# Feed-forward products in 2x2 blocks: seven block products in place of eight

## The chip, the cores and the metric

The kernel runs on one core of one Trainium2 chip. The metric is the device time of one execution in microseconds; the median of three runs is given. The engines are TensorE (PE: matrix products; PEld is its weight load), VectorE (DVE), ScalarE (ACT), GpSimd (POOL) and SyncE (SP, which issues most transfers).

## The reference

A sequence of 512 tokens with 1024 features goes through two blocks of two layers each, A and B, then C and D; the second block puts 16 meta tokens in front (528 tokens). Each layer is a mixer (windowed attention, neighbourhood attention, a gated delta rule with short convolutions, windowed attention with meta tokens) and a feed-forward part, each with a residual sum. The change is in the feed-forward part, whose inner width is 2816:

```python
# layers A and B
gu = h @ w_gate_up[i]                                    # h = rmsnorm(x)
x = x + (jax.nn.silu(gu[..., :D_FF]) * gu[..., D_FF:]) @ w_down[i]
# layers C and D
gate, val = jnp.split(h @ w_up, 2, -1)
gate = causal_dwconv(gate, conv_w)                       # 3 taps along the tokens
x = x + (jax.nn.silu(gate) * val) @ w_down
```

All is in float32.

## The kernel before

Features lie on the 128 partitions and tokens along the free axis, so the stream is 8 tiles `X[j]` of 128 features. Every large product is made in three passes: both operands are split into a high part (an ACT copy to fp32r, which rounds) and a low part (DVE, the operand minus its high part), and `mm3` adds high x high, high x low and low x high in PSUM. `wcols` loads a piece of weights, 4 K chunks of 128 rows by 256 columns, into a tile `raw` (3 buffers) through SP's queue; `wpiece` splits it into `hi` and `lo` (4 buffers each) on ACT (L216) and DVE (L217). `kstep` and `linT` run over the K chunks of one output tile of 128 features. A matrix instruction takes up to 512 columns: 512 tokens go in one piece, 528 tokens in two of 264 (`halves`).

`ffn` goes over the 22 chunks f of the inner width in three groups of 8, 8 and 6. A step f (an up step) loads gate and up columns of all 8 K chunks in two pieces, makes the gate tile and the up tile, scales both by the norm's row scale (L290), in C and D applies three taps to the gate (`conv`, L849), applies silu, multiplies both (L883) and splits the result (`split`, L314 and L315) into `ah`, `al`. After a group, its down products are made for 4 pairs of output tiles `jp` and added to the stream (`resid`, L573). In the first step the norm's sums come between the products (`nj.sums`, `nj.rows`), and what was made before them waits in `Held`. In D the first 16 tokens are left out of all but the taps' input, so the gate has two pieces of 258 and 256 columns, and the up and the down products one of 512.

The tile framework places all waits and orders each engine's instructions by a priority (the order of the program) and its own estimate of when operands and buffers are there; on the chip each engine takes its list in order. The slots (`slot`) are 62 buffers of 544 columns that all stages share; `wk` is a ring of five more. During the feed-forward of A, POOL also issues 96 small transfers that lay out the biases of layer B (`load_biases`, L1057).

Of the kernel before, what the change touches and what calls it, by code (L numbers as in the profile page):

```python
# [9 lines left out]
F32 = mybir.dt.float32  # L10
# [15 lines left out]
GROUPS = [(0, 8), (8, 8), (16, 6)]  # L26
# [6 lines left out]
NHI = 4  # L33
NMM = 3
# [7 lines left out]
TAGS = {'t': (3, ['PT'])}  # L42
# [77 lines left out]
def kernel(ctx: ExitStack, tc: tile.TileContext, stop=None, **a):  # L120
# [41 lines left out]
    def col(w, p, bufs=None):  # L162
        bufs = bufs or (6 if w <= 10 else 2)
# [16 lines left out]
    def load_rows(specs, name, mid=False):  # L180
        """vectors of multiples of 128 as columns of a tile"""
# [22 lines left out]
    # ---------------------------------------------------------------- weights and products  # L204
    def wpiece(loads, nk=4, later=None):
        """loads: (partition lo, partitions, chunk lo, chunks, column lo, columns, dram ap [p, c, n]); the split
        in two goes to the list later, if there is one"""
# [3 lines left out]
        hi = wp.tile([P, 4, 256], F32, tag="hi", name=nm("hi"), bufs=NHI)  # L211
        lo = wp.tile([P, 4, 256], F32, tag="lo", name=nm("lo"), bufs=NHI)
        w = max(n0 + nn for _, _, _, _, n0, nn, _ in loads)

        def parts():
            A.activation(r32(hi[:, :nk, :w]), raw[:, :nk, :w], AF.Copy)  # L216
            V.tensor_tensor(r32(lo[:, :nk, :w]), raw[:, :nk, :w], hi[:, :nk, :w], ALU.subtract)  # L217
# [7 lines left out]
    def wcols(w, k0, runs, nk=4, later=None):  # L225
        """K chunks k0.. of a [K, N] weight, columns in runs [(col, n)]"""
# [7 lines left out]
    def wrows64(w, heads, c0):  # L234
        """4 K chunks, each of a pair of 64-row heads"""
# [16 lines left out]
    def mm3(ps, hi, lo, xh, xl, first, last):  # L252
        PE.matmul(ps, r32(hi), r32(xh), start=first, stop=False)  # L253
        PE.matmul(ps, r32(hi), r32(xl), start=False, stop=False)  # L254
        PE.matmul(ps, r32(lo), r32(xh), start=False, stop=last)  # L255
# [19 lines left out]
    def linN(pcs, xs, o, done):  # L275
        """natural: the 128 tokens from o on the partitions, 256 columns"""
# [10 lines left out]

    def scaled(out, rs, dst):
# [3 lines left out]
    class Held:  # L292
        """products whose scale is still to come; two banks leave at once, one waits"""
# [37 lines left out]
    def rms_cols(accs, wins, rhs, y, eps=None):  # L331
        """y[:, (i, j)] = 1/sqrt(mean square + EPS) of the tokens of window j of accs[i]"""
# [37 lines left out]
    def rows_sb(y, T, name):  # L370
        """1/rms of the tokens (columns y) along the free axis of all partitions, in SBUF"""
# [25 lines left out]
    class Norm:  # L397
        """a norm tile by tile: moving operands (x*g) split in two, then sums() gives 1/rms as columns and rows()
        along the free axis"""
# [38 lines left out]
        def sums_edge(self):  # L438
            """also for the windows shifted by half, the last and the first 64 tokens as one"""
# [19 lines left out]
    class Lag:  # L459
        """finished tiles on to the next norm, each after the one that follows it"""  # L460
# [79 lines left out]
    def load_rows_of(src, ntok, mid=None):  # L540
        """[tokens, 1024] as halves of 128 tokens; mid: more loads, after the first half"""
# [10 lines left out]
    def load_T(nat, ntok, out):  # L552
        """the halves of 128 tokens to 8 tiles [128 features, tokens]"""
# [22 lines left out]
    def spill(X, T):  # L576
        """the stream waits in DRAM until the output projection"""
# [1464 lines left out]
```

## Time and profile before

| | |
|---|---|
| median of 3 runs | 2553.25 us (2552.36 to 2562.22) |
| profiled execution: span from first to last instruction | 2552.4 us, the same as the fastest run's time |
| PE busy | 2520.9 us, 99% |
| DVE busy | 1423.0 us, 56% |
| ACT busy | 968.8 us, 38% |
| POOL busy | 275.8 us, 11% |
| feed-forward stages of A, B, C, D, about | 235 to 602, 820 to 1160, 1580 to 1970, 2177 to 2552 us |

Busy time is the time in which an engine has at least one instruction running. Matrix instructions overlap, so what one costs is read from the distance of starts. A duration on DVE or POOL holds what the instruction waited for inside of the engine.

### The profile page before, as it was taken

The numbers are of one execution on the slowest core, as the hardware profiler recorded it, in microseconds if no ns is written. First come the engines' busy times: TensorE is split into PE (matmuls) and PEld (weight loads), VectorE is DVE, ScalarE is ACT, GpSimd is POOL, SyncE is SP. The second block draws the span as 40 slices with busy tenths as digits, with TensorE's granted clock in tenths as the row PEclk, the third lists the DMA queues.
The fourth block names the chain that finished last, engine by engine and source line by source line (L and its number), as shares of the span: only waits on it lengthen the run. The fifth ranks groups of instructions, "written<-read, shape, count | busy, mean of one in ns | idle before, by whom it ended". The sixth has DMA issues, their size and how long they took to land.

```text
span 2552.4 us, 40552 instructions
## 1 busy us (share of the span) xinstructions
PE 2520.9 (99%) x16222; PEld 2203.4 (86%) x16222; DVE 1423.0 (56%) x2838; ACT 968.8 (38%) x1687; POOL 275.8 (11%) x451
## 2 busy tenths in 40 slices
PE   8999999999999999999999999999999999999999
PEld 6788888888887888888888899999999978988887
DVE  7875434347765434347736556545456775645544
ACT  4764322224654323224423233323234664423322
POOL 3127110003130000004312210000000000000000
PEclk9999999999999999999969999999999999999999
DMA  6144333324221323323301123232324222323232
GB/s 191 40 117 98 101 97 91 99 87 129 83 93 58 99 91 91 99 91 92 103 26 34 42 86 91 83 100 83 99 80 126 62 60 59 91 91 100 93 89 75
DMA packets 333648, 224.80 MB, mean 88 GB/s; under 512 B 43939, under 2 KB 324948, under 8 KB 333460
## 3 DMA queue, kind: packets, MB, share of 16 engines
q1 hardware_dynamic: 327524, 211.82, 28.0%
q0 software_dynamic: 5936, 10.39, 1.5%
q8 instruction: 127, 2.08, 0.3%
q14 instruction: 61, 0.50, 0.1%
HBM read 211.21 MB, written 10.86 MB: 87 GB/s over the span
## 4 chain that ended last, share of the span: by engine, by line
PE 47%; DVE 2%; issue 1%; POOL 0%; ACT 0%; POOLq 0%; DVEq 0%; ACTq 0%
PE mm L253 13%; PE mm L254 13%; PE mm L255 13%; PE pso L1874 1%; PE pss L1454 1%; PE pss L1447 1%; PE pss L1859 1%; PE pss L1431 0%; PE pss L339 0%; PE pss L733 0%; PE pss L1433 0%; PE pso L1879 0%; PE pss L734 0%; DVE xt L1420 0%; PE pss L1854 0%
## 5 line engine op out<-in xcount | busy, mean ns | idle before, releaser
L253 PE MATMUL mm<-xh,hi 128*128 128x264 f32 (+3 forms) x2752 | 916.4, 333 | 7.6 <-ACT xh L393 3.2
L254 PE MATMUL mm<-xl,hi 128*128 128x264 f32 (+3 forms) x2752 | 907.7, 330 | 0.5 <-DVE xl L394 0.5
L255 PE MATMUL mm<-xh,lo 128*128 128x264 f32 (+3 forms) x2752 | 906.1, 329 | 0.0
L217 DVE TENSOR_TENSOR lo<-raw,hi 128x1024 fp32r<-128x1024 f32 (+1 forms) x386 | 464.6, 1204 | 344.8 <-ACT hi L216 342.4
L216 ACT ACTIVATE hi<-raw 128x1024 fp32r<-128x1024 f32 (+1 forms) x386 | 400.2, 1039 | 660.6 <-PE mm L254 579.8
L253 PEld LDWEIGHTS mm<-xh,hi 128*128 128x128 f32 x2752 | 523.2, 190 | 61.7 <-issue 7.5
L254 PEld LDWEIGHTS mm<-xl,hi 128*128 128x128 f32 x2752 | 523.5, 190 | 47.2 <-DVE xl L394 1.3
L255 PEld LDWEIGHTS mm<-xh,lo 128*128 128x128 f32 x2752 | 523.3, 190 | 47.5 <-issue 0.5
L254 PE MATMUL mm<-al,hi 128*128 128x512 f32 (+1 forms) x880 | 308.0, 350 | 0.1
L253 PE MATMUL mm<-ah,hi 128*128 128x512 f32 (+1 forms) x880 | 308.0, 350 | 0.0
L255 PE MATMUL mm<-ah,lo 128*128 128x512 f32 (+1 forms) x880 | 307.8, 350 | 0.0
L573 DVE TENSOR_TENSOR xr<-mm,xr 128x264 f32<-128x264 f32 (+1 forms) x168 | 90.5, 542 | 188.0 <-PE mm L255 187.9
L254 PEld LDWEIGHTS mm<-al,hi 128*128 128x128 f32 x880 | 165.5, 188 | 23.1 <-DVE al L315 0.3
L253 PEld LDWEIGHTS mm<-ah,hi 128*128 128x128 f32 x880 | 165.6, 188 | 22.8
L255 PEld LDWEIGHTS mm<-ah,lo 128*128 128x128 f32 x880 | 165.4, 188 | 22.6
L290 DVE TENSOR_TENSOR gt<-mm,rs 128x512 f32<-128x512 f32 (+3 forms) x128 | 66.3, 518 | 185.5 <-PE mm L255 184.4
L877 ACT ACTIVATE gt<-gt 128x512 f32<-128x512 f32 x44 | 27.8, 632 | 176.6 <-DVE gt L290 176.4
L314 ACT ACTIVATE ah<-ut 128x512 fp32r<-128x512 f32 (+1 forms) x88 | 56.0, 636 | 86.3 <-DVE ut L883 86.3
L846 ACT ACTIVATE cy<-gt,fwcol 128x528 f32<-128x528 f32 (+1 forms) x44 | 32.1, 731 | 147.9 <-DVE gt L290 145.5
L254 PE MATMUL mm<-ol,hi 128*128 128x512 f32 (+1 forms) x256 | 87.6, 344 | 0.0
L255 PE MATMUL mm<-oh,lo 128*128 128x512 f32 (+1 forms) x256 | 87.4, 343 | 0.0
L290 DVE TENSOR_TENSOR ut<-mm,rs 128x512 f32<-128x512 f32 (+1 forms) x108 | 63.7, 590 | 42.2 <-PE mm L255 40.5
(485 smaller groups left out, 3195.2 us busy)
## 6 DMA issues: line engine op xcount, KB each, us to landing
raw<-in_w_gate_up_dram SPq DMA_DIRECT2D x176, 256.0 KB, 3.2
raw<-in_ffn_w_up_dram SPq DMA_DIRECT2D x176, 256.0 KB, 3.4
raw<-in_w_down_dram SPq DMA_DIRECT2D x40, 512.0 KB, 3.4
raw<-in_ffn_w_down_dram SPq DMA_DIRECT2D x40, 512.0 KB, 3.4
raw<-in_mix_w_in_dram SPq DMA_DIRECT2D x28, 512.0 KB, 4.0
raw<-in_w_in_b_dram SPq DMA_DIRECT2D x20, 512.0 KB, 3.6
xr<-xd POOLq DMA_DIRECT2D x16, 264.0 KB, 3.9
raw<-in_w_mem_kv_dram SPq DMA_DIRECT2D x8, 512.0 KB, 3.4
```

The costliest lines, as they stand in the source:

```text
L216: A.activation(r32(hi[:, :nk, :w]), raw[:, :nk, :w], AF.Copy)
L217: V.tensor_tensor(r32(lo[:, :nk, :w]), raw[:, :nk, :w], hi[:, :nk, :w], ALU.subtract)
L253: PE.matmul(ps, r32(hi), r32(xh), start=first, stop=False)
L254: PE.matmul(ps, r32(hi), r32(xl), start=False, stop=False)
L255: PE.matmul(ps, r32(lo), r32(xh), start=False, stop=last)
L290: V.tensor_tensor(dst[:, o:o + n], ps[:, :n], rs[:, o:o + n], ALU.mult)
L314: A.activation(r32(dst_h), src, AF.Copy)
L573: V.tensor_tensor(X[j][:, o:o + n], ps[:, :n], X[j][:, o:o + n], ALU.add)
L846: A.activation(out[:, lo:T], src[:, lo:T], AF.Copy, scale=taps[-1])
L877: A.activation(gt[:, w], gt[:, w], AF.Silu)
L1447: PE.matmul(py[q, h], am[q, h], x[q, h], start=True, stop=True)
L1454: PE.matmul(pzt[q, h], y[q, h], xt[q, h], start=True, stop=True)
```

## The change

With the input in two halves of its features (rows of blocks) and two halves of its tokens (columns), and the weights of a gate tile and an up tile in two halves of K, an up step is a 2x2 product of blocks. It is made by seven block products in place of eight, with sums of blocks before and behind (Winograd's form: four sums of weight blocks, four of input blocks, seven of results). `seven` loads the weights of a step into two `raw` tiles, makes four sums on POOL and splits seven blocks into high and low parts. `Blocks` holds the operands of the other side: `first` and `second` take a chunk of the upper and of the lower half and make four sums (on POOL for the input of the up products, `xb`; on DVE for the activations, `zb`) and seven splits. Each block product is 4 K chunks (3 in the down products) times three passes of 256, 258 or 264 columns. `blocks_to` makes an up step's two tiles, `blocks_add` adds a pair of down tiles to the stream; both keep two sums in PSUM by accumulating a second product onto the first.

The input of the block products is normed beforehand (`normed`), so they need the row scale; the first three steps of each stage (`NPLAIN`) are plain, and the block operands are made during them. Groups are now 6, 6, 6 and 4 chunks, and the down products of a group come after the first up step of the next; those of the last group are plain. The biases of layer B are laid out in DRAM through SP's queue (16 transfers) and loaded as 6 tiles, and the memory keys and values of layer B wait in DRAM until then; small column tiles have 4 buffers where they had 6.

```diff
-GROUPS = [(0, 8), (8, 8), (16, 6)]
+GROUPS = [(0, 6), (6, 6), (12, 6), (18, 4)]
...
+NQT = 3
+NPLAIN = 3
...
-TAGS = {'t': (3, ['PT'])}
+TAGS = {'t': (3, ['PT', 's1', 's2', 's4'])}
...
+    def seven(loads, nk):
+        r0, r1 = [wp.tile([P, 4, 256], F32, tag="raw", name=nm("raw"), bufs=NRAW) for _ in range(2)]
+        for r, ld in zip((r0, r1), loads):
+            for n0, nn, src in ld:
+                nc.sync.dma_start(r[:, :nk, n0:n0 + nn], src)
+        v = lambda t: t[:, :512].rearrange("p (k c) -> p k c", c=P)[:, :nk, :]
+        s1, s2, s4 = [v(slot(x)) for x in ("s1", "s2", "s4")]
+        a_, b_ = (slice(None), slice(0, nk), slice(0, P)), (slice(None), slice(0, nk), slice(P, 256))
+        G.tensor_tensor(s1, r0[b_], r1[b_], ALU.add)
+        G.tensor_tensor(s2, s1, r0[a_], ALU.subtract)
+        G.tensor_tensor(r0[b_], r0[a_], r0[b_], ALU.subtract)
+        G.tensor_tensor(s4, r1[a_], s2, ALU.subtract)
+
+        res = {}
+        for keys, srcs in (((1, 5), (r0[a_], s1)), ((6, 7), (s2, r0[b_])), ((2, 4), (r1[:, :nk, :],)), ((3,), (s4,))):
+            h, l = [wp.tile([P, 4, 256], F32, tag=x, name=nm(x), bufs=NHI) for x in ("hi", "lo")]
+            for i, src in enumerate(srcs):
+                w = slice(i * P, i * P + src.shape[2])
+                split(h[:, :nk, w], l[:, :nk, w], src)
...
+    class Blocks:
...
+        def first(self, k, z):
+            h, l = slot(self.tag), slot(self.tag)
+            v = self.win(z)
+            split(self.part(h, 0), self.part(l, 0), v[:, 0, :])
+            self.eng.tensor_tensor(v[:, 0, :], v[:, 1, :], v[:, 0, :], ALU.subtract)
+            split(self.part(h, 1), self.part(l, 1), v[:, 0, :])
...
+        def second(self, k, z):
+            v, t = self.win(z), self.raw[k]
+            h, l = slot(self.tag), slot(self.tag)
+            split(self.both(h), self.both(l), v)
...
+            self.eng.tensor_tensor(t, v[:, 1, :].unsqueeze(1).to_broadcast([P, 2, self.n]), t, ALU.subtract)
+            h, l = slot(self.tag), slot(self.tag)
+            split(self.both(h), self.both(l), t)
...
+            self.eng.tensor_tensor(v[:, 0, :], v[:, 0, :], t[:, 0, :], ALU.subtract)
+            h = slot(self.tag)
+            split(self.part(h, 0), self.part(h, 1), v[:, 0, :])
...
+    def product(ps, i, ws, bl, more=False):
+        w, b = ws[i], bl.ops[i]
+        for k, ((hi, lo), (h, l)) in enumerate(zip(w, b)):
+            mm3(ps[:, :bl.n], hi, lo, h, l, not more and k == 0, k == len(w) - 1, more)
...
+    def blocks_to(ws, bl, c1, c2):
+        n = bl.n
+        (c11, c12), (c21, c22) = [[c[:, bl.o + i * n:bl.o + (i + 1) * n] for i in range(2)] for c in (c1, c2)]
+        pa, pd = mmps(), bank("s")
+        p1, u2 = [quarter("u")[:, :n] for _ in range(2)]
+        product(pa, 1, ws, bl)
+        A.copy(p1, pa[:, :n])
+        product(pd, 5, ws, bl)
+        A.copy(c22, pd[:, :n])
+        pb = bank("s")
+        product(pb, 6, ws, bl)
+        V.tensor_tensor(u2, pb[:, :n], p1, ALU.add)
+        pc = bank("o")
+        product(pc, 7, ws, bl)
+        V.tensor_tensor(c21, pc[:, :n], u2, ALU.add)
+        G.tensor_tensor(c22, c22, c21, ALU.add)
+        product(pa, 2, ws, bl, more=True)
+        A.copy(c11, pa[:, :n])
+        pe = mmps()
+        product(pe, 4, ws, bl)
+        V.tensor_tensor(c21, pe[:, :n], c21, ALU.add)
+        product(pd, 3, ws, bl, more=True)
+        V.tensor_tensor(c12, pd[:, :n], u2, ALU.add)
...
+    def blocks_add(ws, bl, x1, x2):
...
+        V.tensor_tensor(x22, pd[:, :n], x22, ALU.add)
...
+        V.tensor_tensor(u2, pb[:, :n], p1, ALU.add)
...
+        V.tensor_tensor(w, pc[:, :n], u2, ALU.add)
+        G.tensor_tensor(xb2, xb2, w.unsqueeze(1).to_broadcast([P, 2, n]), ALU.add)
+        G.tensor_tensor(x12, x12, u2, ALU.add)
+        product(pa, 2, ws, bl, more=True)
+        V.tensor_tensor(x11, pa[:, :n], x11, ALU.add)
...
+        V.tensor_tensor(x21, pe[:, :n], x21, ALU.add)
...
+        V.tensor_tensor(x12, pd[:, :n], x12, ALU.add)
...
     def ffn(X, T, nj, wgu, wd, taps, done, lo=0, mid=None):
...
+        lb = max(0, lo - 4)
+        xb = Blocks(4, lb, (T - lb) // 2, "xb", G)
+
+        def normed(k, rs):
+            z = wk("xn")
+            V.scalar_tensor_tensor(z[:, :T], X[k][:, :T], gcol(nj.key, k), rs[:, :T], ALU.mult, ALU.mult)
+            return z
...
+        def up(f, put):
...
+            if f < NPLAIN:
...
+            else:
+                ws = seven([kcols(wgu, 4 * h, 4, [(c, P), (DFF + c, P)]) for h in range(2)], 4)
+                blocks_to(ws, xb, gt, ut)
...
+            put(gt, ut)
+            if f < 2:
+                for k in (2 * f, 2 * f + 1):
+                    xb.first(k, normed(k, state["rs"]))
+                    xb.second(k, normed(k + 4, state["rs"]))
+
+        def down(gi, acts):
...
+                if isinstance(acts, Blocks):
+                    ws = seven([kcols(wd, k0, nk, [(jp * 256, 256)]) for k0 in (f0, f0 + nk)], nk)
+                    blocks_add(ws, acts, X[2 * jp], X[2 * jp + 1])
+                    continue
...
+        before = None
+        for gi, (f0, fn) in enumerate(GROUPS):
+            nk = fn // 2
+            acts = [] if gi == len(GROUPS) - 1 else Blocks(nk, lo, (T - lo) // 2, "zb", V)
...
+            for i in range(fn):
+                up(f0 + i, lambda gt, ut: put(gt, ut, i))
+                if i == 0 and before:
+                    down(*before)
+            before = gi, acts
+        down(*before)
...
+        td = dp.tile([P, 6 * 512], F32, name="TBd")
+        for cc in range(16):
+            nc.sync.dma_start(td[8 * cc:8 * cc + 8, :].rearrange("p (i j) -> p i j", j=32),
+                              scap(15 - cc, [[4608, 8], [48, 96], [1, 32]]))
+            if cc > 1:
+                yield
         for hp in range(6):
-            t = slot("TB")
-            for cc in range(16):
-                G.dma_start(t[8 * cc:8 * cc + 8, :512].rearrange("p (i j) -> p i j", j=32),
-                            scap(hp * 768 + 15 - cc, [[4608, 8], [48, 16], [1, 32]]))
-            TB.append(t)
-            yield
+            TB.append(slot("TB"))
+            nc.sync.dma_start(TB[hp][:, :512], td[:, hp * 512:(hp + 1) * 512])
+        memory_back()
```

## Rows read from the trace of the kernel before

**Rows 1.** The page, part 1: busy time, share of the span and instructions.
```profile
PE 2520.9 (99%) x16222; PEld 2203.4 (86%) x16222; DVE 1423.0 (56%) x2838; ACT 968.8 (38%) x1687; POOL 275.8 (11%) x451
```

**Rows 2.** Windows, feed-forward stages of A, C and D: busy time, instructions, clock, DMA.
```profile
245.00:602.00 357.00, 357.00 (x1549) 290.19 (x1548) 161.64 (x190) 105.96 (x126) 34.21 (x69) 1.00 0.35 102
...
1580.00:1970.00 390.00, 389.87 (x3205) 389.14 (x3204) 210.11 (x329) 127.91 (x160) 4.10 (x8) 1.00 0.32 95
...
2177.00:2552.00 375.00, 370.82 (x2115) 322.74 (x2113) 189.42 (x261) 112.85 (x140) 0.00 (x0) 1.00 0.30 89
```

**Rows 3.** Timeline of PE: starts of 15, 40 and 31 products, first and last.
```profile
599.62 0.39 PE L254 MATMUL mm<-al,hi 128*128 128x512 f32 x1
...
602.84 0.39 PE L253 MATMUL mm<-xh,hi 128*128 128x512 f32 x1
...
626.64 0.28 PE L282 MATMUL mm<-hi,xh 128*128 128x256 f32 x1
...
631.27 0.28 PE L282 MATMUL mm<-hi,xh 128*128 128x256 f32 x1
...
1699.81 0.29 PE L255 MATMUL mm<-ah,lo 128*128 128x264 f32 x1
...
1703.48 0.29 PE L255 MATMUL mm<-ah,lo 128*128 128x264 f32 x1
```

**Rows 4.** Groups of DVE by line and form: count, busy us, mean ns.
```profile
L217 DVE TENSOR_TENSOR lo<-raw,hi 128x1024 fp32r<-128x1024 f32 x368 | 452.4, 1230 | 344.8 <-ACT hi L216 342.4 <-PE mm L284 2.0 <-DMA hwcol<-in_swa_q_norm_w_dram 0.2
...
L315 DVE TENSOR_TENSOR al<-ut,ah 128x512 fp32r<-128x512 f32 x66 | 45.2, 685 | 4.2 <-ACT ah L314 4.2
...
L849 DVE SCALAR_TENSOR_TENSOR cy<-gt,fwcol,cy 128x512 f32<-128x512 f32 x44 | 33.1, 752 | 17.9 <-ACT cy L846 17.2
```

**Rows 5.** Timeline of DVE in a step of A: start us, duration us.
```profile
414.45 0.69 DVE L883 TENSOR_TENSOR ut<-ut,gt 128x512 f32<-128x512 f32 x1
415.06 1.22 DVE L217 TENSOR_TENSOR lo<-raw,hi 128x1024 fp32r<-128x1024 f32 x1
416.19 0.68 DVE L315 TENSOR_TENSOR al<-ut,ah 128x512 fp32r<-128x512 f32 x1
```

**Rows 6.** POOL: a group by form, and one line (min, median, max ns).
```profile
L1351 POOL TENSOR_TENSOR tg<-csts,gg 128x512 f32<-128x512 f32 x4 | 4.1, 1038 | 0.9 <-PE pss L1476 0.9
...
L1443 POOL TENSOR_TENSOR am<-ac,lev x23: 308/731/1701, 1266.9 to 1479.4; 128x256 f32<-128x256 f32 x20, 16x64 f32<-16x64 f32 x3
```

**Rows 7.** Timeline of POOL and of DVE from 1206 us, and line L849 (min, median, max).
```profile
1208.13 12.87 POOL L538 TENSOR_TENSOR xc<-xc,r 128x512 f32<-128x512 f32 x8 [8.85 <-ACT r L534]
...
1206.93 8.27 DVE L849 SCALAR_TENSOR_TENSOR qkv<-cg,cwcol,qkv 128x527 f32<-128x527 f32 x6 [0.19 <-ACT qkv L846]
1215.12 0.76 DVE L290 TENSOR_TENSOR cg<-mm,rs 128x264 f32<-128x264 f32 x2
1216.68 3.17 DVE L849 SCALAR_TENSOR_TENSOR qkv<-cg,cwcol,qkv 128x527 f32<-128x527 f32 x2 [0.81 <-ACT qkv L846]
1219.77 0.42 DVE L290 TENSOR_TENSOR cg<-mm,rs 128x264 f32<-128x264 f32 x1
1220.11 1.45 DVE L849 SCALAR_TENSOR_TENSOR qkv<-cg,cwcol,qkv 128x525 f32<-128x525 f32 x1
...
L849 DVE SCALAR_TENSOR_TENSOR qkv<-cg,cwcol,qkv x36: 745/762/1794, 1206.9 to 1333.2; 128x527 f32<-128x527 f32 x12, 128x526 f32<-128x526 f32 x12, 128x525 f32<-128x525 f32 x12
```

**Rows 8.** Timeline, stage A: its first product, and the row scale's copy.
```profile
234.80 0.40 PE L253 MATMUL mm<-xh,hi 128*128 128x512 f32 x1
...
247.76 0.57 ACT L379 COPY rs<-pss 128x512 f32<-128x512 f32 x1
```

**Rows 9.** Groups of ACT by line and form.
```profile
L216 ACT ACTIVATE hi<-raw 128x1024 fp32r<-128x1024 f32 x368 | 389.2, 1059 | 647.3 <-PE mm L254 566.5 <-issue 49.4 <-PE mm L283 18.2
...
L314 ACT ACTIVATE ah<-ut 128x512 fp32r<-128x512 f32 x66 | 41.8, 633 | 45.3 <-DVE ut L883 45.3
```

**Rows 10.** The page, part 6: issues, KB each, median us to landing.
```profile
raw<-in_w_gate_up_dram SPq DMA_DIRECT2D x176, 256.0 KB, 3.2
```

More of the change, by code (lines that the diff above doesn't have):

```diff
@@ L210, in wpiece @@
             nc.sync.dma_start(raw[p0:p0 + pn, c0:c0 + cn, n0:n0 + nn], src)
-        hi = wp.tile([P, 4, 256], F32, tag="hi", name=nm("hi"), bufs=NHI)
-        lo = wp.tile([P, 4, 256], F32, tag="lo", name=nm("lo"), bufs=NHI)
+        hi, lo = [wp.tile([P, 4, 256], F32, tag=x, name=nm(x), bufs=NHI) for x in ("hi", "lo")]
         w = max(n0 + nn for _, _, _, _, n0, nn, _ in loads)
         def parts():
-            A.activation(r32(hi[:, :nk, :w]), raw[:, :nk, :w], AF.Copy)
-            V.tensor_tensor(r32(lo[:, :nk, :w]), raw[:, :nk, :w], hi[:, :nk, :w], ALU.subtract)
+            split(hi[:, :nk, :w], lo[:, :nk, :w], raw[:, :nk, :w])
         if later is None:
@@ L250, in wrows64, with mm3 @@
         return wpiece(loads)
[L252 to L255, printed above, removed]
+    def mm3(ps, hi, lo, xh, xl, first, last, more=False):
+        PE.matmul(ps, r32(hi), r32(xh), start=first, stop=False, skip_group_check=more)
+        PE.matmul(ps, r32(hi), r32(xl), start=False, stop=False, skip_group_check=more)
+        PE.matmul(ps, r32(lo), r32(xh), start=False, stop=last, skip_group_check=more)
     def kstep(out, pcs, k, t, xs, first, last):
@@ L286, in linN @@
         done(ps)
+    def seven(loads, nk):
[16 more added lines that the diff above has]
+                split(h[:, :nk, w], l[:, :nk, w], src)
+            for i, key in enumerate(keys):
+                res[key] = [(h[:, k, i * P:(i + 1) * P], l[:, k, i * P:(i + 1) * P]) for k in range(nk)]
+        return res
@@ L766, in memory_kv, with memory_back @@
                 yield from linN(pcs, xs, t * P, done)
+            if li:
+                d = dp.tile([5 * P, 512], F32, name="memd")
+                for i, t in enumerate([x for pair in kst for h in pair for x in [h[2]]] + [vs]):
+                    nc.sync.dma_start(d[i * P:(i + 1) * P, :], t[:, :512])
+                memK.append(d)
+                memV.append(None)
+                continue
             memK.append(kst)
             memV.append(vt)
+    def memory_back():
+        d = memK[1]
+        t = [slot("memb") for _ in range(5)]
+        for i, x in enumerate(t):
+            nc.sync.dma_start(x[:, :512], d[i * P:(i + 1) * P, :])
+        memK[1] = [[(t[2 * i + hh][:, :256], t[2 * i + hh][:, 256:512]) for hh in range(2)] for i in range(2)]
+        memV[1] = [t[4][:, :256], t[4][:, 256:512]]
     def out_proj(piece, get, T, done, early):
@@ L849, in conv, with kcols @@
             V.scalar_tensor_tensor(out[:, o:T], src[:, o - d:T - d], taps[n - 1 - d], out[:, o:T], ALU.mult, ALU.add)
+    def kcols(w, k0, nk, runs):
+        out, at = [], 0
+        for c, n in runs:
+            out.append((at, n, w[k0 * P:(k0 + nk) * P, c:c + n].rearrange("(c p) n -> p c n", p=P)))
+            at += n
+        return out
     def ffn(X, T, nj, wgu, wd, taps, done, lo=0, mid=None):
@@ L854, in ffn @@
         lg = max(0, lo - 2)
-        for gi, (f0, fn) in enumerate(GROUPS):
-            acts = []
-            for f in range(f0, f0 + fn):
-                c = f * P
-                if mid is not None and f >= MID and (f - MID) % MSTEP == 0:
-                    next(mid, None)
+        w = slice(lo, T)
+        lb = max(0, lo - 4)
[4 more added lines that the diff above has]
+            return z
+        state = {}
+        def up(f, put):
+            c = f * P
+            if mid is not None and f >= MID:
+                next(mid, None)
+            gt, ut = wk("gt"), wk("ut")
+            if f < NPLAIN:
                 pcs = [wcols(wgu, 4 * h, [(c, P), (DFF + c, P)]) for h in range(2)]
-                gt, ut = wk("gt"), wk("ut")
-                w = slice(lo, T)
                 if f == 0:
@@ L889, in ffn, with put @@
                     j = 2 * jp + t
-                    fin = done if gi == len(GROUPS) - 1 else resid(X)
-                    run(linT(pcs, t, acts, T, lambda out, j=j, fin=fin: fin(j, out), fn, lo=lo, wide=j == 0))
+                    run(linT(pcs, t, acts, T, lambda out, j=j: done(j, out), fn, lo=lo, wide=j == 0))
+        before = None
+        for gi, (f0, fn) in enumerate(GROUPS):
+            nk = fn // 2
+            acts = [] if gi == len(GROUPS) - 1 else Blocks(nk, lo, (T - lo) // 2, "zb", V)
+            def put(gt, ut, i):
+                if isinstance(acts, list):
+                    ah, al = slot("ah"), slot("al")
+                    V.tensor_tensor(ut[:, w], ut[:, w], gt[:, w], ALU.mult)
+                    split(ah[:, w], al[:, w], ut[:, w])
+                    acts.append((ah, al))
+                elif i < nk:
+                    z = slot("z")
+                    V.tensor_tensor(z[:, w], ut[:, w], gt[:, w], ALU.mult)
+                    acts.first(i, z)
+                else:
+                    V.tensor_tensor(ut[:, w], ut[:, w], gt[:, w], ALU.mult)
+                    acts.second(i - nk, ut)
+            for i in range(fn):
[4 more added lines that the diff above has]
+        down(*before)
     def dump(X, T, off=0):
```

68 lines of the change are left out of this document (50 added, 18 removed).

## The prediction

> **What bounds the kernel now.** I read the page's busy shares first: TensorE (PE) is busy 99% of the span of 2552.4 us, VectorE (DVE) far less [rows 1]. Shares mix stages, so next the windows by stage: in the feed-forward stages of the layers A, C and D, PE is busy for the whole window, while DVE is busy 162 of 357 us in A and 210 of 390 us in C, and GpSimd (POOL) 34 and 4 us [rows 2]. The stage of layer B looks like that of A. So PE sets the pace in exactly the stages that are rewritten, and DVE has slack. What a product costs is the distance of starts in the matmul timeline, not its duration, since they overlap: 14 steps of 512 columns in 3.22 us, 0.230 each; 39 steps of 256 columns in 4.63 us, 0.119 each; 30 steps of 264 columns in 3.67 us, 0.1223 each [rows 3]. So narrow products cost per column nearly what wide ones do, and halving the width loses 3%, not more.
>
> **What it removes on PE.** One up step (two output tiles, 8 K chunks, three passes) has 48 products of 512 columns in A and B, 48 x 0.230 = 11.04 us. The block form has 7 x 4 x 3 = 84 of 256 columns, 84 x 0.119 = 9.97. In C, 96 x 0.1223 = 11.74 becomes 84 x 0.1223 = 10.27. In D, half are pairs of some 257 columns: 24 x 0.230 + 48 x 0.119 = 11.23 becomes 84 x 0.119 = 9.97. 19 of 22 steps change. A pair of output tiles of a down group of 6 chunks has 36 x 0.230 = 8.28 us (C: 72 x 0.1223 = 8.80); the block form has 63 products, 7.48 (C: 7.70). There are 12 such pairs. PE work saved: A and B 19 x 1.07 + 12 x 0.80 = 29.9 us each, C 19 x 1.47 + 12 x 1.10 = 41.1, D 19 x 1.26 + 9.6 = 33.5; 134 us in all. This would be the gain if PE stayed the bound.
>
> **What it adds, in an up step.** Every block sum and every split now goes through DVE, ScalarE (ACT) and POOL. On DVE I count what one instruction adds to a run of them: 512 columns 0.61 us and 1024 columns 1.13 (starts at 414.45, 415.06, 416.19 [rows 5]), where the durations are 0.685 and 1.23 [rows 4]; 256 columns 0.34 (two evacuations of 0.42 in 0.76 us [rows 7]). The weights need low parts of five 512-column blocks and one of 1024: 5 x 0.61 + 1.13 = 4.18, before 2.26. The gate times up product is 0.61 as before. The activations' block operands take, over a pair of chunks, three times 256 in the first half, and three times 512 and two times 256 in the second: (1.02 + 2.51) / 2 = 1.77, before 0.61. That is 6.56 us of DVE instructions with both inputs in SBUF. Four evacuations of 256 columns from PSUM add 1.36. POOL gets four sums of 512 columns at 1.04 and one of 256 at 0.73 [rows 6]: 4.89, where it had nothing.
>
> **Why these two sums add up.** DVE and POOL look like two engines in parallel, each below PE's 9.97. The trace says they are not, for these instructions. From 1208 us POOL runs eight sums of 512 columns back to back (1.04 alone) while DVE has tap instructions of two SBUF inputs (0.75 alone): DVE's stretch up to 1.79, 0.75 + 1.04, and POOL's eight take 12.87 us instead of 8.3 [rows 6, 7]. Seven taps begin in those 12.87 us (of the first six the two before 1208.13 don't count), and each is 0.08 shorter in a run: 7 x 0.67 + 8 x 1.04 = 13.0. So one holds the other up, and the sum of both is the time. The three PSUM evacuations in there kept 0.42 and cost nothing [rows 7]. So a step takes at least 6.56 + 4.89 = 11.45 us (floor), and 12.81 if no evacuation lies under POOL (in line). Before: 11.04. The seventh of PE's work is saved, and DVE with POOL becomes the bound.
> By the Trainium skill (SBUF — State Buffer, Who interferes with whom) a DVE instruction with two SBUF inputs and a GpSimd one that reads SBUF exclude each other for the whole instruction, and one with a single SBUF input is left alone. The trace agrees but for 0.08 us of a DVE instruction. With full durations the floor would be 12.3 us. The same skill (GPSIMD Engine Reference, Engine selection) sends elementwise sums to VectorE; the rows give 0.61 there against 1.04, so the placement on POOL takes 2.1 us more of the shared time in a step than needed.
>
> **The sum by stage**, floor / middle / in line. I take the middle: the evacuations rode free in the one stretch shown, but here the DVE also has to wait for PE's last product of a step.
> Up, A and B: 11.45 / 12.13 / 12.81 against 11.04. C adds two taps of 0.75: 13.0 / 13.7 / 14.4 against 11.74. D: 12.95 / 13.6 / 14.3 against 11.23. In the last four steps the activations are split plainly, 1.16 us less. Of the 19 steps 15 are full.
> Down, a pair of tiles with 3 + 3 chunks: widths 384 and 768 aren't in the trace; between the rows they take 0.475 and 0.87 on DVE, 0.89 on POOL. DVE 5 x 0.475 + 0.87 = 3.25, POOL 4 x 0.89 + 1.04 + 0.73 = 5.33, floor 8.58; six evacuations 2.04, in line 10.62; middle 9.6. Against 8.28 (C 8.80).
> A and B: 15 x 1.09 - 4 x 0.07 + 12 x 1.32 = +32 us each (bounds 15 x 0.41 - 4 x 0.75 + 12 x 0.30 = +7 and 15 x 1.77 + 4 x 0.61 + 12 x 2.34 = +57). C: 15 x 1.96 + 4 x 0.80 + 12 x 0.80 = +42 (+17 to +68). D: 15 x 2.40 + 4 x 1.24 + 12 x 1.32 = +57 (+32 to +82).
> Start of each stage: the block operands of the input need the norm's row scale, which lands 13.5 us into the stage (234.80 to 248.33 [rows 8]). Three plain steps, 33.1 us and some 2 for the norm's sums, end 21.5 us later. In these lie, for each of four pairs of chunks, DVE 2 x 0.75 + 0.68 + 1.56 and POOL 0.73 + 1.04 + 0.73, 6.2 us, so 25; and 7.1 of the plain steps' own (weights 2.26, products 3 x 0.61, first block operands 3 x 1.02). 32.1 in 21.5 leaves the first block product 10.6 us late; 42 us in four stages. Bounds 4 and 20 each, by how far the chain from ACT to DVE to POOL and back overlaps.
> Sum: 2 x 32 + 42 + 57 + 42 = +205; bounds 2 x 7 + 17 + 32 + 16 = +79 and 2 x 57 + 68 + 82 + 80 = +344.
>
> **What I cost at nothing.** ACT: a step has five splits at 0.63, one at 1.06 [rows 9], three copies of 256 columns, the activation and 1.2 of operands, under 8 us in a step of 12. DMA: the weights' bytes and issues in the changed steps are the same, and a load lands in 3.2 us [rows 10]; without that cover it is the rival on buffers. The biases of layer B go by a DRAM tile on SP's queue, not POOL's, and five tiles of memory keys and values go to DRAM and back: all of it inside stage A, whose buffers would have to run dry for it to count. Fewer small column tiles: a wait between tiny instructions, below 1 us each in attention. The last group of four chunks is plain in its down products and costs what it did.
>
> **Rivals.** 1. POOL's sums don't hold DVE up (the pair in the rows shared more than the port, say, or POOL reads these blocks quickly). Then PE stays the bound in all steps: DVE alone needs 7.9 of 9.97 us in A and 9.5 of 10.27 in C. 134 us less, some 3 us lost at each start: 2552 - 134 + 12 = 2430. For it: the page's shares, and DVE's slack. Against: 1.79 us taps. It decides once a sum holds DVE up for about 0.28 us less than the 0.94 it takes on average: 95 + 72 + 12 sums in each stage, 716 in all, and 205 / 716 = 0.29 brings the time back to before.
> 2. It cancels: sums below the floor in A and B by overlap, above in C and D, within 0.5%.
> 3. Buffers bind as well. Three raw tiles serve two per step, and the first is held until its difference has been split. From its release to that of the next: the load 3.2, three POOL sums at 1.04 with a DVE instruction of 0.61 before each, 4.95, the high part 0.63, the low part 0.61 behind a POOL sum of 1.04: 10.4 us, and then the wait for a high/low tile that PE still reads. Four such tiles are one step's set. If this adds 1.9 us to 76 steps and 1.5 to 48 pairs, 2757 + 216 = 2970.
>
> **How the numbers follow.** The profiled execution's span is 2552.4, next to the fastest run's 2552.36 and 0.85 below the median of 2553.25, so the sum is one on the median within 1 us: 2552.4 + 205 = 2757. Chances: shared port as bound, 2631 to 2896, 0.72; a little below that and still slower 0.04; rival 3 0.08; rival 1 0.11; rival 2 0.05. Faster by over 0.5% (about what a measurement of this kernel can tell from no change) 0.11, within it 0.05, slower 0.84. The range goes from 2570 to 2970, which leaves out rival 1, rival 2 and half of rival 3; the likeliest one's own is 2631 to 2896.
>
> **What would show it.** Right: in the feed-forward windows PE's busy share falls well below 1, PE waits for DVE's low parts; POOL's sums of 512 columns last well over 1.04 and DVE's splits over 0.69 on average; DVE plus POOL busy comes close to the window. An up step in the middle of A takes 11.5 to 12.8 us, in C 13.0 to 14.4; some 10 us of idle PE before the first block product. Wrong, if matmuls of 256 columns don't start 0.119 us apart when fed, if POOL's sums keep 1.04 beside DVE's splits, or if PE waits for loads.

## The result, and the profile after

The changed kernel takes 2859.52 us in the median of four runs (2851.23 to 2865.14), against 2552.81 for the kernel before on the same chip: a ratio of 1.1189, 95% interval 1.1156 to 1.1222. The forecast was 2757 us, slower with a chance of 0.84, and a range of 2570 to 2970. Sign and mechanism held. The size was half as large again, +307 in place of +205, between the middle and the upper bound (+344).

The page of the changed kernel, part 1, answers to [rows 1]:
```profile
PE 2542.0 (89%) x18454; PEld 2316.2 (81%) x18454; DVE 2204.5 (77%) x3981; ACT 1321.9 (46%) x2663; POOL 1164.6 (41%) x1071
```
PE fell from 99% to 89%. PE's busy time did not fall although its work did. At least part of the reason is half clock, which makes a matmul count as busy for longer: at about 440.5 us, where the granted clock falls from 2.4 to 1.2 GHz, the duration of a 256-column matmul goes from 0.28 to 0.41 us and the distance of starts from 0.12 to 0.22, and the mean granted clock of the whole execution went from 0.986 to 0.949. The windows of the four feed-forward stages, A to D, show where it waits, and answer to [rows 2] (columns as there: PE, PEld, DVE, ACT, POOL busy, clock, DMA share, GB/s):
```profile
245.00:690.00 445.00, 376.11 (x2622) 350.73 (x2622) 354.58 (x518) 196.45 (x375) 252.22 (x231) 0.94 0.32 94
897.00:1335.00 438.00, 371.00 (x2621) 343.72 (x2619) 382.66 (x524) 203.36 (x397) 253.71 (x193) 0.96 0.27 79
1765.00:2190.00 425.00, 346.66 (x2555) 333.06 (x2556) 366.17 (x514) 197.12 (x367) 228.17 (x177) 0.94 0.28 82
2404.00:2863.00 459.00, 383.77 (x2715) 358.90 (x2714) 386.98 (x551) 205.32 (x386) 235.98 (x179) 0.94 0.25 75
```
PE has gone from the whole window to 82 to 85% of it, DVE from about half to 80 to 87%, POOL from next to nothing to more than half. What PE waits for, in the list of waits (total us, times, longest us):
```profile
PE pss L255 <- DVE lo L451: 83.6, 65, 4.6
PE mm L255 <- DVE lo L451: 75.3, 48, 3.7
```
So it waits for the low parts that DVE makes. The groups of DVE and of POOL by form (count, busy us, mean ns) answer to [rows 4] and [rows 6]:
```profile
L451 DVE TENSOR_TENSOR lo<-raw,hi 128x1024 fp32r<-128x1024 f32 x228 | 284.5, 1248 | 67.9 <-ACT hi L450 60.7 <-DMA raw<-in_w_out_dram 6.5 <-PE mm L255 0.5
L451 DVE TENSOR_TENSOR lo<-s,hi 128x512 fp32r<-128x512 f32 x228 | 219.6, 969 | 17.7 <-ACT hi L450 15.9
L451 DVE TENSOR_TENSOR lo<-raw,hi 128x512 fp32r<-128x512 f32 x154 | 185.0, 1202 | 9.2 <-ACT hi L450 7.5
L386 DVE TENSOR_TENSOR ut<-pso,u 128x256 f32<-128x256 f32 x38 | 15.9, 417 | 3.3 <-PE pso L255 1.8
```
```profile
L305 POOL TENSOR_TENSOR s<-raw,s 128x512 f32<-128x512 f32 x76 | 126.7, 1667 | 5.7 <-ACT zb L450 3.4 <-DVE lo L451 2.3
L304 POOL TENSOR_TENSOR raw<-raw 128x512 f32<-128x512 f32 x76 | 126.0, 1657 | 0.0
```
The low parts of 512 columns, 0.685 us in [rows 4], now take 0.97 to 1.20 on average; the evacuations, with one input in PSUM, keep 0.417; POOL's sums, 1.04 in [rows 6], take up to 1.67. One place in stage B shows how a mean of 1.2 comes about; first the timeline of DVE, then that of POOL over the same stretch (start us, us):
```profile
1078.55 0.69 DVE L352 TENSOR_TENSOR z<-ut,z 128x512 f32<-128x512 f32 x1
1079.28 0.69 DVE L451 TENSOR_TENSOR zb<-ut,zb 128x512 fp32r<-128x512 f32 x1
1080.00 1.41 DVE L357 TENSOR_TENSOR ut<-ut,z 128x256 f32<-128x256 f32 x1
1081.33 1.78 DVE L451 TENSOR_TENSOR zb<-z,zb 128x512 fp32r<-128x512 f32 x1
1083.04 1.48 DVE L451 TENSOR_TENSOR zb<-ut,zb 128x256 fp32r<-128x256 f32 x1
1084.44 0.41 DVE L383 TENSOR_TENSOR u<-pss,u 128x256 f32<-128x256 f32 x1
```
```profile
1079.36 1.77 POOL L302 TENSOR_TENSOR s<-raw,raw 128x512 f32<-128x512 f32 x1 [4.63 <-DVE z L352]
1081.20 1.36 POOL L303 TENSOR_TENSOR s<-s,raw 128x512 f32<-128x512 f32 x1
1082.53 1.71 POOL L304 TENSOR_TENSOR raw<-raw 128x512 f32<-128x512 f32 x1
1084.20 1.44 POOL L305 TENSOR_TENSOR s<-raw,s 128x512 f32<-128x512 f32 x1
```
(The bracket is the engine's idle time before the row and what ended it.) Here a DVE instruction with two SBUF inputs that finds a sum running takes up to 1.1 us longer than without one: 512 columns 1.78 in place of 0.69, 256 columns 1.48 in place of the 0.42 that the same line takes at 440.12 us, where no sum runs. The one at 1079.28, which runs already when the first sum starts, keeps its 0.69, and the sum takes 1.77. While the four sums run, the two engines take turns. The last row, an evacuation, meets a sum as well and keeps its 0.41.

Two windows of four up steps each in stage B, and one of a whole group there (six up steps and four pairs of down tiles, from one gate activation to that six later):
```profile
1064.60:1116.40 51.80, 43.55 (x314) 42.05 (x315) 50.09 (x62) 25.52 (x53) 28.10 (x20) 0.90 0.25 75
1182.00:1234.00 52.00, 41.35 (x324) 39.08 (x324) 50.36 (x62) 25.48 (x52) 27.53 (x20) 1.00 0.25 74
...
1052.10:1169.30 117.20, 100.45 (x756) 95.37 (x756) 104.76 (x138) 52.18 (x105) 72.47 (x54) 0.96 0.28 81
```
An up step takes 12.95 and 13.0 us on average, a little over the upper bound of the prediction (12.81), and DVE is busy for 97% of it: held, but with hardly a gap. The clock was 0.90 in one window and 1.00 in the other, and the time is the same, so half clock doesn't set the pace in these windows.

### The profile page after: what moved, and what is told of

Its sections match the earlier page's. It is cut to its first block, busy times and chain, and to the rows that moved or that the text cites. A ratio compares the mean times of both kernels' runs of the same rounds, so it can differ in the third digit from the quotient of the medians.

```text
span 2863.1 us, 48858 instructions
## 1 busy us (share of the span) xinstructions
PE 2542.0 (89%) x18454; PEld 2316.2 (81%) x18454; DVE 2204.5 (77%) x3981; ACT 1321.9 (46%) x2663; POOL 1164.6 (41%) x1071
## 4 chain that ended last, share of the span: by engine, by line
PE 38%; DVE 31%; POOL 10%; issue 10%; ACT 5%; DMA 5%; SPq 0%; POOLq 0%; DVEq 0%; ACTq 0%
DVE lo L451 12%; PE mm L253 8%; PE mm L254 7%; PE mm L255 7%; DVE zb L451 4%; POOL s L302 2%; POOL s L303 2%; POOL raw L304 2%; ACT hi L450 2%; DMA raw<-in_ffn_w_down_dram 2%; DVE cy L1002 1%; POOL s L305 1%; DVE z L1085 1%; PE pss L869 1%; PE pss L255 1%
## 5 line engine op out<-in xcount | busy, mean ns | idle before, releaser
L451 DVE TENSOR_TENSOR lo<-raw,hi 128x1024 fp32r<-128x1024 f32 (+3 forms) x526 | 591.9, 1129 | 82.9 <-ACT hi L450 72.8
L450 ACT ACTIVATE hi<-raw 128x1024 fp32r<-128x1024 f32 (+3 forms) x526 | 422.1, 813 | 273.0 <-PE mm L254 107.5
L451 DVE TENSOR_TENSOR lo<-s,hi 128x512 fp32r<-128x512 f32 (+1 forms) x372 | 328.8, 890 | 63.8 <-ACT hi L450 62.0
L253 PE MATMUL mm<-xh,hi 128*128 128x264 f32 (+3 forms) x1080 | 362.3, 336 | 15.5 <-DVE gt L425 4.4
L254 PE MATMUL mm<-xl,hi 128*128 128x264 f32 (+3 forms) x1080 | 352.9, 327 | 0.7 <-DVE xl L530 0.6
L255 PE MATMUL mm<-xh,lo 128*128 128x264 f32 (+3 forms) x1080 | 351.3, 326 | 0.0
L253 PE MATMUL mm<-xb,hi 128*128 128x256 f32 (+2 forms) x912 | 267.1, 293 | 42.8 <-ACT u L378 27.9
L253 PE MATMUL pss<-xb,hi 128*128 128x256 f32 (+2 forms) x912 | 272.6, 299 | 30.9 <-ACT hi L450 15.8
L254 PE MATMUL pss<-xb,hi 128*128 128x256 f32 (+2 forms) x912 | 270.2, 296 | 2.8 <-DVE xb L451 2.6
L254 PE MATMUL mm<-xb,hi 128*128 128x256 f32 (+2 forms) x912 | 263.8, 289 | 2.2 <-DVE xb L451 2.2
L254 PEld LDWEIGHTS mm<-xl,hi 128*128 128x128 f32 x1080 | 210.7, 195 | 15.6 <-DVE xl L530 2.5
L255 PEld LDWEIGHTS mm<-xh,lo 128*128 128x128 f32 x1080 | 210.5, 195 | 14.2 <-issue 0.5
```

The source lines that it names most:

```text
L253: PE.matmul(ps, r32(hi), r32(xh), start=first, stop=False, skip_group_check=more)
L254: PE.matmul(ps, r32(hi), r32(xl), start=False, stop=False, skip_group_check=more)
L255: PE.matmul(ps, r32(lo), r32(xh), start=False, stop=last, skip_group_check=more)
```

## The experiments

All are edits of the changed kernel, except the two whose names begin with "before". "Group in B" is the group shown last, at its own place in each trace.

| kernel | us, median | profiled span | group in B |
|---|---|---|---|
| before | 2552 | 2552.4 | 99.4 by PE's terms of the prediction |
| the changed kernel | 2859.5 | 2863.1 | 117.2 |
| sums_dve | 2697.2 | 2686.1 | 102.4 |
| results_dve | 2846.8 | 2851.6 | 117.5 |
| no_sums | 2520.9 | 2519.1 | 88.6 |
| lone_sums | 2941.8 | 2939.6 | 124.5 |
| narrow | 2606.6 | 2586.9 | 95.5 |
| raw4 | 2800.8 | 2794.7 | 112.5 |
| both_dve | 2671.0 | 2672.9 | 99.0 |
| sums_dve_spread | 2662.1 | 2656.8 | 103.2 |
| best | 2600.7 | 2591.9 | 98.9 |
| best_b | 2552.0 | 2543.7 | 97.3 |
| before_pool4 | 2755.2 | 2752.4 | |
| before_dve4 | 2587.3 | 2585.6 | |

My theory was the shared time of DVE and POOL; the rivals were the order of POOL's list (the sums of the next step wait there behind the addition to `c22`, which waits for the seventh product), the raw buffers, and half clock.

**sums_dve.** The weight sums move to VectorE.
```diff
-        G.tensor_tensor(s1, r0[b_], r1[b_], ALU.add)
+        V.tensor_tensor(s1, r0[b_], r1[b_], ALU.add)
...
```
(and the same for the three sums below it)

> The four sums of the weight blocks of seven run on VectorE in place of GpSimd; the output stays the reference's. Shared-time theory (GpSimd's sums and VectorE's tensor-tensor work hold each other up, so that their times add): the sums cost VectorE about 0.7 us each in place of the 1.27 to 1.67 us that GpSimd takes, and the subtractions of split go back from 0.97-1.2 us to about 0.7, so a step of the up-projection falls from some 13.5 to about 11.5 us: total 2600 to 2720. Rival, GpSimd's order (the sums wait in GpSimd's list behind the addition to c22, and the splits wait for the sums): the sums no longer queue there, so the time falls as well, to about 2650 to 2720; lone_sums tells the two apart. Rival, half clock (the losses are stretches at half clock that any stall causes): falls less, 2780 to 2850.

162 us come back, more than half of the loss, ratio to before 1.0572 (1.049 to 1.0654). The group of low parts from sums is back at its old duration:
```profile
L451 DVE TENSOR_TENSOR lo<-s,hi 128x512 fp32r<-128x512 f32 x228 | 156.4, 697 | 0.0
```

**results_dve.** Only the additions to result quarters move to VectorE, so that nothing in POOL's list waits for a product.
```diff
-        G.tensor_tensor(c22, c22, c21, ALU.add)
+        V.tensor_tensor(c22, c22, c21, ALU.add)
...
-        G.tensor_tensor(xb2, xb2, w.unsqueeze(1).to_broadcast([P, 2, n]), ALU.add)
-        G.tensor_tensor(x12, x12, u2, ALU.add)
+        V.tensor_tensor(xb2, xb2, w.unsqueeze(1).to_broadcast([P, 2, n]), ALU.add)
+        V.tensor_tensor(x12, x12, u2, ALU.add)
```


> The additions of result quarters (c22 in the up-projection, xb2 and x12 in the down-projection) run on VectorE in place of GpSimd; the output stays the reference's. GpSimd's list then holds nothing that waits for a product. Shared-time theory: 0.3 to 0.5 us a step come back at most, 2810 to 2850. Rival, GpSimd's order (the next step's four weight sums stand behind the addition to c22, which waits for the seventh product): the sums start when their load lands, 1 to 2 us a step earlier, and the time falls to 2650 to 2750.

13 us, and a group in B of 117.5 against 117.2. The order of POOL's list is worth these 13 us at most.

**no_sums.** The sums are left out; raw blocks stand in for them.
```diff
-        for keys, srcs in (((1, 5), (r0[a_], s1)), ((6, 7), (s2, r0[b_])), ((2, 4), (r1[:, :nk, :],)), ((3,), (s4,))):
+        for keys, srcs in (((1, 5), (r0[a_], r1[b_])), ((6, 7), (r1[a_], r0[b_])), ((2, 4), (r1[:, :nk, :],)), ((3,), (r0[a_],))):
```


> The four sums of the weight blocks are left out: the seven products take raw blocks in their place, so that the seven products no longer make up the reference's product. Everything else, splits and loads and result sums, stays. Shared-time theory: without the sums VectorE has some 10 us of a step and TensorE some 10 as well, so the time is near 2450 to 2520, faster than before. Rival, raw buffers or stage starts bind by themselves (a load of 3.2 us, then splits, from only three buffers): stays above 2600. Rival, half clock: depends on stalls that go away with the sums, 2430 to 2550.

2520.9, just above what was expected (2450 to 2520). Its group in B is bound by PE, at 88.6 us against 6 x 9.97 + 4 x 7.48 = 89.7 by the prediction's PE terms, so the price of the products was right:
```profile
962.40:1051.00 88.60, 88.60 (x750) 88.60 (x750) 77.11 (x138) 51.90 (x105) 14.77 (x14) 1.00 0.37 108
```
Even with no weight sums at all the seven products gain only 1.2% over before (ratio 0.9880, 0.9827 to 0.9933).

**lone_sums.** POOL makes the same sums, and nothing reads them.
```diff
+        s3 = v(slot("s1"))
...
-        G.tensor_tensor(r0[b_], r0[a_], r0[b_], ALU.subtract)
+        G.tensor_tensor(s3, r0[a_], r0[b_], ALU.subtract)
...
```
(and the sources of the splits as in no_sums)

> GpSimd still makes the four sums of the weight blocks, but into tiles that nothing reads; the splits take the raw blocks, so the seven products no longer make up the reference's product. The same GpSimd work, with nothing waiting for its results except the buffers it reads. Shared-time theory: the sums still take VectorE's time, 4 x 1.0 to 1.3 us a step; little of the 310 us comes back, 2750 to 2850. Rival, GpSimd's order (the chain load, sums, splits, products sets the pace): the chain is cut, so the time falls to near that of no_sums, 2450 to 2600.

Cutting the chain brought nothing back. It even lost 82 us more, which neither theory had. The up steps are as in the changed kernel, 51.5 us for four; the loss is in the down pairs. The waits of ACT say what is late there:
```profile
ACT hi L451 <- DMA raw<-in_ffn_w_up_dram: 113.9, 32, 10.4
...
ACT hi L451 <- DMA raw<-in_w_gate_up_dram: 95.1, 26, 10.0
ACT hi L451 <- DMA raw<-in_w_down_dram: 79.2, 17, 9.2
```
Loads arrive later than the splits want them. That the raw tiles are held longer, by POOL's late sums and by all splits, fits this but was not tried by itself.

**narrow.** The order of the sums stays, and so do their wait for the load and the splits' wait for them. They cover an eighth of the columns and are made in place, so they need no tiles of their own.
```diff
-        G.tensor_tensor(s1, r0[b_], r1[b_], ALU.add)
...
+        na, nb = (slice(None), slice(0, nk), slice(0, 16)), (slice(None), slice(0, nk), slice(P, P + 16))
+        G.tensor_tensor(r1[nb], r0[nb], r1[nb], ALU.add)
+        G.tensor_tensor(r1[na], r1[nb], r0[na], ALU.subtract)
+        G.tensor_tensor(r0[nb], r0[na], r0[nb], ALU.subtract)
+        G.tensor_tensor(r0[nb], r1[na], r0[nb], ALU.subtract)
```
(and the sources of the splits as in no_sums)

> The four weight sums stay on GpSimd, in the same order and in front of the same splits, but each covers 16 of the 128 columns of its block and is made in place in the raw buffers; the seven products no longer make up the reference's product. The chain load, sums, splits, products and GpSimd's order are kept; GpSimd's time for the sums falls to a fraction. Shared-time theory, which the first four runs favour: the time falls to within 60 us of the run without sums (2521), so 2520 to 2580. Rival, the chain through GpSimd's list: the sums still wait behind the addition to c22 and the splits for them, so most of the 340 us between that run and the changed kernel stays, 2700 or more.

2606.6 (2589.0 and 2624.2), 26 above the expected range: 86 over no_sums in the medians, 68 in the profiled spans, of the 339 that lie between no_sums and the changed kernel. POOL's busy time is 202.7 us over no_sums (666.3 against 463.6), so this too is partly shared time. The chain is worth about a quarter of the loss at most.

**raw4.** Four raw tiles in place of three.
```diff
-NSLOT = 62
+NSLOT = 60
...
-NRAW = 3
+NRAW = 4
```


> Four raw buffers in place of three (and 60 slots in place of 62, to make the room), so that both loads of the next step can land while this step's raw blocks are held. Rival 3 of the prediction (raw buffers bind as well): 30 to 100 us come back, 2760 to 2830. Shared-time theory: the loads land earlier, but VectorE's and GpSimd's time is what fills the step: 2830 to 2860.

59 us come back: the buffers do bind as well, beside the shared time. In part this is again the shared time, since with a fourth tile the sums run at other places. Counted in the timelines of both engines, 4 of 16 evacuations (1.64 of their 6.57 us) lie under POOL's instructions in the window 1064.60:1116.40 above, and 9 of 16 (3.73 of 6.63 us) in the same four steps here, which take 48.3 us in place of 51.8.

**both_dve** joins sums_dve and results_dve.

> Both the weight sums and the additions of result quarters run on VectorE; GpSimd then has only the block differences of xb. The output stays the reference's. Against the run with the sums alone on VectorE (2697): if VectorE's own time fills the steps there, an addition of 128x256 costs it about 0.4 us either way (held up by GpSimd's 1.1 us, or its own), so 2680 to 2710. If the waits for GpSimd's additions that this run's trace still shows (20 us at c21, 10 at xr) are on the path, 2660 to 2675.

26 us better than sums_dve, in the range expected if the waits for POOL's additions are on the path; POOL is empty of the new work except for the block differences of `xb`.

**sums_dve_spread** gives the block operands of the input four plain steps in place of two.
```diff
-            if f < 2:
-                for k in (2 * f, 2 * f + 1):
-                    xb.first(k, normed(k, state["rs"]))
-                    xb.second(k, normed(k + 4, state["rs"]))
+            if f < 4:
+                xb.first(f, normed(f, state["rs"]))
+                xb.second(f, normed(f + 4, state["rs"]))
```
(with NPLAIN = 5)

> Weight sums on VectorE, the blocks of xb made over four plain steps (one pair of tiles each) in place of two, and the first seven-product step is step 5 in place of 3. The output stays the reference's. If the start of a stage is late because the block operands of xb crowd VectorE in two steps (start steps of 15 to 17 us against 11 before, some 15 to 20 us a stage), 30 to 60 us come back against 2697: 2640 to 2670. If the start is late for the loads or the first sums, it moves with the step: 2690 to 2710.

35 us, within what was expected: these operands do crowd the first steps of a stage. From the first to the eighth gate activation stage A takes 123.1 us where sums_dve takes 132.3, and stage B 116.0 against 124.3. The run also makes two steps fewer of each stage in blocks, and no run separates the two.

**before_pool4.** The kernel before, with four sums beside each weight piece that no one reads.
```diff
+            G.tensor_tensor(out, raw[:, :2, :], in1, ALU.add)
+            for _ in range(3):
+                G.tensor_tensor(out, in1, in1, ALU.add)
```


> The kernel before, all of its products unchanged, with four more GpSimd sums of 512 columns for each weight piece of the feed-forward stages (two pieces a step), into a scratch tile that nothing reads; the first of the four reads the piece's raw tile. The output stays the reference's. A piece has 5.5 us of TensorE; VectorE is busy some 2.4 of these and GpSimd would be 4.2 with its sums at 1.04. Shared-time theory: 2.4 + 4.2 to 5.1 is 6.6 to 7.5 us a piece, so GpSimd's sums last 1.3 us or more, the low parts of the splits over 1.5 in place of 1.23, and the time rises to 2750 to 3050 with no block product in the kernel. Rival, no holding (the loss comes from the chain through sums and splits): nothing waits for these sums, 2552 to 2570.

2755.2, ratio 1.0793 (1.0755 to 1.0830), in a kernel without a block product. The groups of DVE and of POOL by form, and a window of stage B:
```profile
L226 DVE TENSOR_TENSOR lo<-raw,hi 128x1024 fp32r<-128x1024 f32 x368 | 583.9, 1588 | 427.8 <-ACT hi L225 425.2 <-PE mm L264 2.0
L325 DVE TENSOR_TENSOR al<-ut,ah 128x512 fp32r<-128x512 f32 x66 | 92.1, 1396 | 7.9 <-ACT ah L324 7.8
...
L212 POOL TENSOR_TENSOR x<-x 128x512 f32<-128x512 f32 x816 | 1104.8, 1354 | 62.4
```
```profile
930.00:1020.00 90.00, 81.89 (x343) 65.59 (x344) 54.26 (x48) 26.22 (x33) 85.30 (x61) 0.96 0.29 88
```
DVE's low parts went from 1.230 to 1.588 and from 0.685 to 1.396 [rows 4], and POOL's sums take 1.354 in place of 1.04. At 1.04 four of them would fit into a piece's 5.5 us of PE. No instruction reads them, but the next load into a raw tile waits for the first of its four, which reads the tile (247 waits, 1265 us in all); so POOL's pace becomes that of the step. POOL fills the window with 61 sums, so a piece of four takes 90 / 15.25 = 5.90 us. Its DVE work with both inputs in SBUF is 1.13 + (0.61 + 0.61) / 2 = 1.74 a piece (the weights' low part, and half a step's gate product and low part), and 1.74 + 4 x 1.04 = 5.90. The expectation, 6.6 at least, had counted the evacuations in. Here they are free: all in the window lie under POOL's sums. In stage C, with two taps of 0.67 more in a step, the same sum gives 13.1 us a step, and 12.56 was measured (2030.59 to 2043.15 us); why it is 4% less there stays open. Part of the 200 us isn't this: stage A alone lost some 90, and in the kernel before the biases of layer B are loaded from POOL's own queue, behind the added sums.

**before_dve4.** The same sums on VectorE.

> The same with the four scratch sums of each piece on VectorE behind its split. The output stays the reference's. VectorE would be busy 2.4 + 4 x 0.61 = 4.9 us of 5.5 a piece. Shared-time theory: this still fits, 2552 to 2600. If VectorE's busy share is not what counts, but any sum ahead of a split delays it, 2650 or more.

2587.3, ratio 1.0135 (1.010 to 1.017). The same work costs 35 us there and 203 on POOL (stage A's 90, with its biases, included).

**best** joins both_dve, the spread start and four raw tiles.

> All that helped so far together: weight sums and result sums on VectorE, xb's blocks over four plain steps, four raw buffers. The output stays the reference's. From 2671 (both on VectorE), some 35 us less for the spread start and 10 to 40 for the fourth raw buffer: 2590 to 2630, slower than before still, since VectorE's work in a step (about 10 us) is near that of TensorE.

2600.7, still 1.9% slower than before (1.0141 to 1.0234). In its group in B, DVE is busy 96.6 of 98.9 us, now with its own work:
```profile
954.20:1053.10 98.90, 95.22 (x758) 92.17 (x757) 96.61 (x193) 54.15 (x103) 0.00 (x0) 0.98 0.33 97
```

**best_b** keeps that version in stage B alone; A, C and D go back to eight products.

> The same version of the blocks in the feed-forward stage of layer B alone; the stages of A, C and D make the eight plain products of the kernel before. The output stays the reference's. With both sums on VectorE stage B was some 3 us slower than before from its first activation to that of C, and the spread start and the fourth buffer may give 5 to 20: 2535 to 2555. If it comes out below 2545 the blocks pay where VectorE has room.

2552.0 in ten runs, against 2552.5 in thirteen; ratio 1.0011 (0.9990 to 1.0033), not below the 2545 that would have shown a gain. No version that makes all of its sums beats the kernel before.

## Why the prediction was right, and where its size was off

**Shared time of DVE and POOL: right.** The sums cost what they take from both engines: before_pool4 shows the holding with nothing that reads the sums, 5.90 us a piece in B by the prediction's own per-instruction figures; sums_dve takes more than half of the loss away. Rival 1 (2430 us) is out. By the Trainium skill (SBUF — State Buffer, Who interferes with whom) a DVE instruction with two SBUF inputs contends with a GpSimd one that reads SBUF, and one with a single SBUF input, outside DVE's two-port modes, does not; the timeline's 0.42 that became 1.48, and the evacuations' 0.417, agree.

**Price of a block product: right.** 88.6 us a group in no_sums, against 89.7.

**Steps in the middle of a stage: the term was undersized.** The prediction's "middle" between floor and in line let half of the evacuations lie under POOL's sums. For a group in B the prediction's figures give 6 x 11.45 + 4 x 8.58 = 103.0 (floor), 111.2 (middle) and 6 x 12.81 + 4 x 10.62 = 119.3 (in line). Measured: 117.2, 87% of the way from floor to in line. The term that was too small is the one behind the sentence that begins "I take the middle: the evacuations rode free in the one stretch shown": the sums come in a block of four, and of a step's four evacuations on DVE few meet it; in the timeline above the block lasts from 1079.36 to 1085.64, and only the evacuation at 1084.44 lies in it. In the four steps from 1064.60 us a quarter of the evacuations lie under POOL, not half: 11.45 + 0.75 x 1.36 = 12.47, and 0.43 us of idle DVE a step makes 12.90 of the 12.95 measured. With four raw tiles it is over half, and a group takes 112.5, near the middle. So the count of raw tiles, rival 3 at a chance of 0.08, is part of the same miss: not as the loop that it was priced at (+216), but 59 us. The sign given for an up step failed in A, 11.5 to 12.8 against means of four of 15.6 us in the second group and 13.1 in the third; in C, 13.0 to 14.4, it held with 14.2 in both.

**Start of a stage: undersized.** I gave 10.6 us for each, with bounds of 4 and 20. The timelines of ACT show the first and the fourth gate activation of stage A in the kernel before, in the changed kernel, and in no_sums:
```profile
249.75 0.63 ACT L877 ACTIVATE gt<-gt 128x512 f32<-128x512 f32 x1
...
275.95 0.63 ACT L877 ACTIVATE gt<-gt 128x512 f32<-128x512 f32 x1 [4.19 <-DVE gt L290]
```
```profile
252.65 0.63 ACT L1052 ACTIVATE gt<-gt 128x512 f32<-128x512 f32 x1
...
299.14 0.63 ACT L1052 ACTIVATE gt<-gt 128x512 f32<-128x512 f32 x1 [0.74 <-DVE gt L394]
```
```profile
252.89 0.63 ACT L1047 ACTIVATE gt<-gt 128x512 f32<-128x512 f32 x1
...
291.65 0.63 ACT L1047 ACTIVATE gt<-gt 128x512 f32<-128x512 f32 x1 [0.81 <-DVE gt L389]
```
That is 26.2, 46.5 and 38.8 us. In the kernel before, the fourth activation stands between the gate product and the up product, 24 x 0.230 = 5.5 us ahead of the end of its step; to the same place it is 31.7. So the start is 14.8 us late, and 7.1 without the weight sums: the operands of the input cost less than I gave, but the weight sums of the first block step fall into the same crowded stretch, 7.7 us that I had not counted. By the same reckoning (half a step of the kernel before is 5.9 us in C and 5.6 in D) the four stages start 14.8, 15.0, 17.3 and 13.1 late, 60 in place of 42. With the sums on DVE (sums_dve) it is 39.0, 7.3 late. With the operands spread over four plain steps as well the first block step is the sixth: 60.3 us, against 48.4 + 5.5 in the kernel before, 6.4 late. The rest of the miss, 311 - 60 = 251 against 163, lies behind the starts, mostly in the steps; an estimate from the activations and PE's prices puts some 20 us of it between one stage's last activation and the next one's first.

**Half clock: not priced.** Stretches at half clock show in all four stages after, and hardly in [rows 2]. The two windows in B above, where DVE is busy for 97%, say that it cost nothing there. One group does show more: from the eighth gate activation of stage A to the fourteenth it takes 131.1 us, the next six take 115.5, and in this window neither DVE nor POOL is full while the clock is 0.89:
```profile
385.00:475.00 90.00, 73.23 (x522) 70.78 (x521) 56.94 (x96) 37.53 (x74) 38.19 (x33) 0.89 0.30 81
```
At 1.2 in place of 2.4 GHz for 22% of 90 us, PE loses up to 10 us there, by estimate. Without sums this group is slow too (112.7, then 94.9), and in best it nearly isn't (104.3, then 98.1), with a fourth raw tile among its edits. What starts it stays open.

**Costed at nothing: ACT and DMA.** ACT is under 50% in every stage. The count of raw tiles, which decides how early a load can start, was not free: a fourth one gives 59 us back.

**DVE plus POOL close to the window** was a poor sign to name. Held time counts as busy on both, so they add up to 177 of 117 us in the group above.

## What to carry to other kernels

An algebra that trades products for sums moves work from PE to DVE; count the sums, the splits and the evacuations against PE's step before counting products, because an idle share on DVE is the whole budget. Two-input sums on POOL are no way round it when DVE has two-input work of its own: add both engines' times (right to 4% in the two stages compared here), and leave the instructions that read PSUM out only as far as they fall under POOL's sums. Price the first steps of a stage with everything that falls into them, including the first instructions of the steady part.

## What the runs showed of the hardware

A DVE instruction with two SBUF inputs that waited for a POOL sum of 512 columns grew by up to 1.1 us, at 512 columns (0.69 to 1.78) as at 256 (0.42 to 1.48), so short ones suffer most in proportion. An evacuation of PSUM kept its 0.41 beside a sum. The same 1088 sums of 512 columns cost 35 us of the kernel's time on DVE and 203 on POOL, some 90 of these in stage A, where the biases' transfers stood behind them. The granted clock was 0.90 in one window of four steps in B and 1.00 in another, and they took 51.8 and 52.0 us: half clock did not lengthen steps in which DVE was busy for 97%.
